# Up projection: eight of 22 steps as seven block products, with weight sums added by transfers

## The chip, the cores and the metric

The kernel runs on one core of one Trainium2 chip. Time is the device time of one launch in microseconds, given as the median of several runs. The core has a matrix engine (TensorE, PE in the profile, with its weight loads as PEld), a vector engine (VectorE, DVE), a scalar engine (ScalarE, ACT), GpSimd (POOL) and SyncE (SP), which issues most of the transfers. Each engine takes its own instructions strictly in the order of its list.

## The reference

One layer over 512 latent rows of width 1024, with 256 context rows: a modulated RMSNorm, one input projection that feeds a two-way state-space mixer and a windowed attention, both merged by gates and projected; then a second modulated RMSNorm, a gated convolutional feed-forward of width 2816, and a final norm.

```python
mod = jax.nn.silu(c) @ w_mod[l] + b_mod[l]
sh1, sc1, gt1, sh2, sc2, gt2 = jnp.split(mod[:, None, :], N_MOD, axis=-1)
...
x = x + gt1 * o_lat          # o_lat = (g_ssd * (y_ssd @ w_o_ssd) + g_att * (y_att @ w_o_att)) @ w_out
x = x + gt2 * conv_ffn(modulate(x, norm2_g[l], sh2, sc2), w_up[l], ffn_conv_w[l], ffn_conv_b[l], w_down[l])
...
def conv_ffn(h, w_up, conv_w, conv_b, w_down):
    u = dwconv_centred(h @ w_up, conv_w, conv_b)      # three taps along the rows
    a, b = u[..., :D_FF], u[..., D_FF:]
    return (jax.nn.silu(a) * b) @ w_down
```

## The kernel before

All products run in two parts for precision: a 32-bit operand is split into a high part (a cast on ACT, `whi`) and a low part (a subtraction on DVE, `wlo`), and each product is three matmuls: high by high, input-low by high, input-high by low. `gemm` issues them for k = 0 to 7 in that order, so the third matmul of a step is the first that reads `wlo`. A weight step is 128 output columns: a load of 512 KB into one of three buffers (`wraw`, issued on SP), the cast, the subtraction (`split`), and 24 matmuls of 512 columns.

The program is one list of steps. `run` walks it and issues the load and the split of a weight one weight ahead of the step that uses it. A scheduler then sets the final order on each engine, except where a block is pinned by hand (`manual_schedule`), or where a manual dependency ties an instruction behind another. `weave` spreads the second list of steps evenly among the first.

The stages that the change touches are these, in the order of the program.
- From the entry on, DRAM to DRAM transfers issued by POOL form sums of down-projection weights (`SUMS`), each a copy and a transfer that adds, tied behind splits by `sum_step`. The down projection already runs as seven block products on them.
- The output projection of the mixer: steps os0 to os7, then out0 to out4 (`out_step`) and `out_last`, which does steps 5, 6 and 7 in halves of 256 rows. Each out step evicts `x` (x1 = old x plus gain times product, on DVE), squares it on ACT and adds the square to `q` on DVE. The squares feed the root of norm 2 (`rs`, on POOL) and its spread over partitions on PE.
- The modulation vectors: `m_step` i forms products of an already loaded weight (`wm`) with the silu of c on DVE, two for every 512 KB (`tm`). Four steps make one group of 512 outputs; groups 2 to 5 are summed over partitions by four transposes on PE and a reduction on DVE, while groups 6 and 7 are summed by `fold`: the tile is stored to DRAM and halved eight times by transfers that add, each waiting for the one before, all on POOL.
- The up projection: 22 steps (`up_step`) of two weights, a (gate) and b, 48 matmuls of 512 columns. Each half is convolved over rows (`conv`: an ACT activation and two DVE sums), a goes through silu, and the product stays for the down projection. `f_sums` forms that projection's column sums. `x1_turn` transposes x1 by blocks and stores it.

What set the amounts woven before:

```python
+ weave([os_step(o) for o in range(3, 8)], msteps[10:18])
+ weave([out_step(o) for o in range(5)], msteps[18:24])
...
weave([up_step(t) for t in range(18)], msteps[24:]) + [up_step(t) for t in range(18, NFF)],
```

## Time and profile before

| | us |
|---|---|
| median of 3 runs (lowest, highest) | 1214.6 (1213.96, 1215.82) |
| the profiled execution | 1214.44 |
| its span | 1212.7 |
| PE busy | 1204.0 |
| DVE busy | 917.3 |
| ACT busy | 684.6 |
| POOL busy | 265.6 |

The mean granted clock of the profiled execution is 0.999. Timeline rows give start, duration, engine, line of the kernel, operation, output<-inputs and count, with the idle time before it and what ended it in brackets. A matmul's own duration is modelled and overlaps the next one's; the distance of two starts is what it costs. Groups of instructions by line give busy time, mean ns of one, and idle time before. Rows of transfers give queue, count, size and the median us from issue to landing.

### The profile page before, as it was taken

The page shows a single profiled execution, that of the slowest core. Times are in us where ns is not written, and L with a number is a line of the kernel's source. Part 1 is how long each engine was busy: PE and PEld are TensorE (multiplying, and loading weights), DVE is VectorE, ACT ScalarE, POOL GpSimd, SP SyncE. Part 2 cuts the span into 40 slices and gives each one's busy share as a digit, 9 for nine tenths or more (in the row PEclk, how much of TensorE's full clock was granted, in tenths as well). Part 3 has the DMA queues.
Part 4 walks back from the last instruction along what each step waited for, and adds up shares of the span by engine and source line. Part 5 has one row for each costly group of instructions (what it writes and reads, how often), then busy time and mean ns, then how long its engine had stood idle before and what let it go on. Part 6 is the DMA issues. An engine that isn't in the chain of part 4 may idle for free.

```text
span 1212.7 us, 17847 instructions
## 1 busy us (share of the span) xinstructions
PE 1204.0 (99%) x6429; PEld 1006.4 (83%) x6429; DVE 917.3 (76%) x1476; ACT 684.6 (56%) x1269; POOL 265.6 (22%) x274
## 2 busy tenths in 40 slices
PE   9999999999999999999999999999999999999998
PEld 6798888888878878788787888888988888888886
DVE  5857887888565588788887977677677777668787
ACT  4657887778543457476575674223544343436654
POOL 0000121100102546265382780000200100110021
PEclk9999999999999999999999999999999999999999
DMA  9655789844747736567467568677265634436652
GB/s 368 257 144 185 161 232 269 169 136 137 170 153 228 229 106 197 162 161 189 147 175 265 178 232 267 223 251 236 53 163 146 200 113 139 130 106 225 213 186 97
DMA packets 129417, 224.30 MB, mean 185 GB/s; under 512 B 27336, under 2 KB 70640, under 8 KB 129328
## 3 DMA queue, kind: packets, MB, share of 16 engines
q1 hardware_dynamic: 115248, 195.61, 51.5%
q0 software_dynamic: 13792, 27.27, 10.0%
q8 instruction: 51, 0.84, 0.3%
q14 instruction: 38, 0.31, 0.1%
q10 hardware_dynamic: 288, 0.27, 0.1%
HBM read 196.17 MB, written 45.02 MB: 199 GB/s over the span
## 4 chain that ended last, share of the span: by engine, by line
PE 93%; DMA 2%; DVE 1%; POOL 1%; issue 1%; ACT 1%; DVEq 0%; POOLq 0%; ACTq 0%
PE acc L238 18%; PE acc L241 18%; PE acc L239 18%; PE score L979 3%; PE po L1028 3%; PE pt L1015 2%; PE mis L582 2%; PE mis L1759 2%; PE mis L1602 2%; DMA xs_d<-xb 2%; PE mis L2310 2%; PE mis L2311 2%; PE mis L2309 2%; PE mis L1767 1%; PE acc L2310 1%; PE acc L2311 1%
## 5 line engine op out<-in xcount | busy, mean ns | idle before, releaser
L184 DVE TENSOR_TENSOR wlo<-wraw,whi 128x1024 fp32r<-128x1024 f32 (+1 forms) x115 | 148.3, 1289 | 87.9 <-ACT whi L183 84.7
L183 ACT CAST whi<-wraw 128x1024 fp32r<-128x1024 f32 (+1 forms) x115 | 120.3, 1047 | 154.0 <-PE acc L239 104.6
L238 PE MATMUL acc<-hlh,whi 128*128 128x512 f32 x472 | 192.8, 409 | 0.0
L241 PE MATMUL acc<-hlh,wlo 128*128 128x512 f32 x472 | 185.6, 393 | 0.0
L239 PE MATMUL acc<-hll,whi 128*128 128x512 f32 x472 | 185.0, 392 | 0.0
L238 PE MATMUL acc<-mh,whi 128*128 128x512 f32 x368 | 143.3, 389 | 0.0
L239 PE MATMUL acc<-ml,whi 128*128 128x512 f32 x368 | 143.2, 389 | 0.0
L241 PE MATMUL acc<-mh,wlo 128*128 128x512 f32 x368 | 143.2, 389 | 0.0
L241 PEld LDWEIGHTS acc<-hlh,wlo 128*128 128x128 f32 x472 | 88.6, 188 | 19.9 <-issue 0.5
L238 PEld LDWEIGHTS acc<-hlh,whi 128*128 128x128 f32 x472 | 88.8, 188 | 17.6 <-issue 2.8
L239 PEld LDWEIGHTS acc<-hll,whi 128*128 128x128 f32 x472 | 88.9, 188 | 17.4 <-issue 2.2
L241 PEld LDWEIGHTS acc<-mh,wlo 128*128 128x128 f32 x368 | 69.1, 188 | 14.4
L239 PEld LDWEIGHTS acc<-ml,whi 128*128 128x128 f32 x368 | 69.1, 188 | 14.3
L238 PEld LDWEIGHTS acc<-mh,whi 128*128 128x128 f32 x368 | 69.1, 188 | 14.2
L164 POOL DMA_DIRECT2D dsum<-wdn x24 | 25.3, 1119 | 194.4 <-DVE wlo L1112 183.7
L988 DVE CUSTOM_DVE_ANT_0 p<-score,winm,nsink 128x512 f32<-128x512 f32 (+1 forms) x64 | 51.9, 810 | 15.3 <-PE score L979 13.8
L995 ACT ACTIVATE p<-p,mneg 128x512 f32<-128x512 f32 (+1 forms) x64 | 49.8, 778 | 15.4 <-DVE mneg L988 14.8
L813 DVE SCALAR_TENSOR_TENSOR tm<-wraw,csil,tm 128x512 f32<-128x512 f32 x56 | 45.8, 818 | 12.2 <-DMA wraw<-wm 11.4
L1023 DVE TENSOR_TENSOR ptl<-pt,pth 128x512 fp32r<-128x512 f32 x72 | 47.5, 686 | 8.5 <-ACT pth L1019 7.7
L238 PE MATMUL acc<-hch,whi 128*128 128x256 f32 x176 | 53.2, 302 | 0.0
L1112 DVE TENSOR_TENSOR wlo<-wraw,whi 128x1024 fp32r<-128x1024 f32 x30 | 36.7, 1223 | 18.3 <-ACT whi L1109 18.0
L241 PE MATMUL acc<-hch,wlo 128*128 128x256 f32 x176 | 49.8, 283 | 0.0
(458 smaller groups left out, 3056.9 us busy)
## 6 DMA issues: line engine op xcount, KB each, us to landing
wraw<-wup SPq DMA_DIRECT2D x44, 512.0 KB, 3.9
dsum<-wdn POOLq DMA_DIRECT2D x24, 704.0 KB, 8.5
wraw<-wm SPq DMA_DIRECT2D x32, 512.0 KB, 4.2
fb<-cs_d SPq DMA_DIRECT2D x32, 512.0 KB, 7.1
wraw<-wx SPq DMA_DIRECT2D x24, 512.0 KB, 4.1
wm<-wm SPq DMA_DIRECT2D x16, 512.0 KB, 8.3
wraw<-wz SPq DMA_DIRECT2D x16, 512.0 KB, 5.0
far<-us_d SPq DMA_DIRECT2D x32, 256.0 KB, 5.3
```

The costliest lines, as they stand in the source:

```text
L183: F["cast"] = S.copy(hi[:, :n], r[:, :n])
L184: F["sub"] = V.tensor_tensor(lo[:, :n], r[:, :n], raw(hi[:, :n]), ALU.subtract)
L238: T.matmul(ps, wh, xh[:, k0 + k, :], start=a, stop=False)
L239: T.matmul(ps, wh, xl[:, k0 + k, :], start=False, stop=False)
L241: T.matmul(ps, wl, xh[:, k0 + k, :], start=False, stop=b)
L813: V.scalar_tensor_tensor(acc, r[:, u * 512 : u * 512 + 512], sc, acc, ALU.mult, ALU.add)
L979: T.matmul(ps[:, o : o + len(z) * P], Q[h][:, b * P : (b + 1) * P], k[:, j, z[0] * P : (z[-1] + 1) * P], start=v == 0 and o % 512 in (0, P ...
L988: V.tensor_tensor_reduce(p[:, :w], d["ps"][i][:, o0 : o0 + w], m, op0=ALU.add, op1=ALU.min, scale=1.0, scalar=nsink[:, h : h + 1], accum_o ...
L995: S.activation(p, p, AF.Exp, bias=d["mneg"][:, i : i + 1], scale=-1.0, accum_out=d["den"][:, i : i + 1])
L1023: V.tensor_tensor(d["ptl"][x], d["pt"][x], raw(d["pth"][x]), ALU.subtract)
L1028: T.matmul(d["po"], vst[:, cols[x], j, :], d[y][x], start=x == 0 and y == "pth", stop=x == c - 1 and y == "ptl")
L1112: sum_step(V.tensor_tensor(d["w"][1], d["r"], raw(d["w"][0]), ALU.subtract), 1 + (4 <= g < 12))
```

## The change

Eight of the 22 up steps (t = 5 to 12) are written as seven products of half-size blocks (weights halved along the contraction and between a and b, inputs along the contraction and the rows): 84 matmuls of 256 columns in place of 48 of 512. Four block sums of weights are formed by adding transfers in DRAM, in three chains that are issued in turn, together with the down sums, two behind each split from the entry on; the host adds a second layout of the same weights (`wup7`) that has no arithmetic in it. Eight of the down sums' transfers (`LATE`) stand behind splits of up steps past 13. Four block sums of the inputs are formed by 7 DVE passes and split by 4 casts and 4 subtractions, in pieces pinned behind splits of up steps 0 to 4. The steps of seven products have their order written out by hand for all four engines, and multiply the two halves on POOL. The column sums of steps up to 17 are formed later, in larger pieces.

The other steps move to make room: the os stage now has modulation steps 10 to 19 (was 10 to 17), the five out steps have 20 to 27 and four of the eight transposes of x1 (was 18 to 23 and none), and up steps 14 to 17 have modulation steps 28 to 31 and the other four transposes (the former were woven into up steps 0 to 17, with the transposes).

In the lists below lines have the numbers of each kernel. On DVE, around the eviction of out step 2 (before, L1984, then after, L2043): `wlo` is the split of the next weight, `mod` and `a` the modulation vector, `tm` the modulation products, `ta<-x` the transposes of x1.

```order
L1984 SCALAR_TENSOR_TENSOR x_7775<-acc,g1h,te 128x512
L184 TENSOR_TENSOR wlo<-wraw,whi 128x1024
L1933 TENSOR_TENSOR q_7777<-q_7777,tc 128x512
L813 SCALAR_TENSOR_TENSOR tm<-wraw,csil,tm 128x512 x4
L1984 SCALAR_TENSOR_TENSOR x_7775<-acc,g1h,te 128x512
```

```order
L2043 SCALAR_TENSOR_TENSOR x_7800<-acc,g1h,te 128x512
L882 TENSOR_REDUCE mod_95<-mis 128x4
L1992 TENSOR_TENSOR q_7802<-q_7802,tc 128x512
L883 TENSOR_TENSOR mod_95<-mod_95,vec 128x4
L870 TENSOR_SCALAR tm<-wraw,csil 128x512
L1981 SCALAR_TENSOR_TENSOR a_7804<-mod_95,vec 128x8
L872 SCALAR_TENSOR_TENSOR tm<-wraw,csil,tm 128x512
L2409 STREAM_TRANSPOSE ta<-x_7800 128x512
L224 TENSOR_TENSOR wlo<-wraw,whi 128x1024
L872 SCALAR_TENSOR_TENSOR tm<-wraw,csil,tm 128x512 x2
L2409 STREAM_TRANSPOSE ta<-x_7800 128x512
L2043 SCALAR_TENSOR_TENSOR x_7800<-acc,g1h,te 128x512
```

Before, the split is the first row behind the eviction; now seven rows stand between. The same holds further on, for out step 3 with one row and for the split of `wlast` with four.

On POOL, around the two roots of norm 2 (`rs`; `ml` is the low part of the normed input), before and after:

```order
L296 TENSOR_TENSOR rs<-ms,phalf 128x4
L296 TENSOR_TENSOR rs<-ms,phalf 128x2
L2026 TENSOR_TENSOR ml<-ta,mh 128x256 x3
L296 TENSOR_TENSOR rs<-ms,phalf 128x2
L2026 TENSOR_TENSOR ml<-ta,mh 128x256 x5
L789 DMA fold_765<-tm 128x512
```

```order
L355 TENSOR_TENSOR rs<-ms,phalf 128x4
L848 DMA fold_768<-tm 128x512
L850 DMA fold_768<-fold_768 256x128
L850 DMA fold_768<-fold_768 128x128
L850 DMA fold_768<-fold_768 64x128
L850 DMA fold_768<-fold_768 32x128
L850 DMA fold_768<-fold_768 16x128
L355 TENSOR_TENSOR rs<-ms,phalf 128x2
L850 DMA fold_768<-fold_768 16x64
L2085 TENSOR_TENSOR ml<-ta,mh 128x256
L850 DMA fold_768<-fold_768 16x32
L2085 TENSOR_TENSOR ml<-ta,mh 128x256
```

The fold of group 6, which stood behind all of norm 2, now has six of its transfers ahead of the first root of two columns.

On DVE, from the end of up step 17 to the split of step 18's first weight (`tc` is the convolution of half b), before and after:

```order
L184 TENSOR_TENSOR wlo<-wraw,whi 128x1024
L2059 SCALAR_TENSOR_TENSOR tc<-acc,vec,tc 128x511
L2060 SCALAR_TENSOR_TENSOR tc<-acc,vec,tc 128x511
L2072 TENSOR_TENSOR fx_8982<-tb,tc 128x512
L2050 SCALAR_TENSOR_TENSOR fx_8981<-fx_8981,fx_8982 128x256
```

```order
L2141 SCALAR_TENSOR_TENSOR tc<-acc,vec,tc 128x511
L2142 SCALAR_TENSOR_TENSOR tc<-acc,vec,tc 128x511
L2154 TENSOR_TENSOR fx_9057<-tb,tc 128x512
L872 SCALAR_TENSOR_TENSOR tm<-wraw,csil,tm 128x512 x2
L224 TENSOR_TENSOR wlo<-wraw,whi 128x1024
```

The split stood ahead of the second half's convolution, and now stands behind it and the last two modulation products.

```diff
-    SUMS = []
-    for j, first_, more in (
-        (4, wdn[0], wdn[2]), (1, wdn[2], wdn[3]), (2, DSUMS[4], wdn[3]), (5, DSUMS[2], wdn[1]),
-    ):
-        cols = [slice(q * DK * P, (q + 1) * DK * P) for q in range(4)]
-        SUMS += [(DSUMS[j][:, c], first_[:, c], {}) for c in cols]
-        SUMS += [(DSUMS[j][:, c], more[:, c], dict(accum_op=ALU.add, max_dma_last_dim=DK * P)) for c in cols]
+    US = dpool.tile([P, 4, len(SEVEN) * 512], F32, name="usum")
+    SUMS, LATE = [], []
+
+    def added(o, x, y):
+        return [(o, x, {}), (o, y, dict(accum_op=ALU.add, max_dma_last_dim=DK * P))]
+
+    def in_turn(runs, n):
+        out, live = [], []
+        runs = list(runs)
+        while runs or live:
+            while runs and len(live) < n:
+                live.append(list(runs.pop(0)))
+            for r in live:
+                out.append(r.pop(0))
+            live = [r for r in live if r]
+        return out
+
+    RUNS = []
+    for q in range(4):
+        c = slice(q * DK * P, (q + 1) * DK * P)
+        two, four = DSUMS[2][:, c], DSUMS[4][:, c]
+        RUNS.append(added(four, wdn[0][:, c], wdn[2][:, c]) + added(two, four, wdn[3][:, c]))
+        RUNS.append(added(DSUMS[1][:, c], wdn[2][:, c], wdn[3][:, c]))
+        LATE.append(added(DSUMS[5][:, c], two, wdn[1][:, c]))
+    for i in range(0, len(SEVEN), 2):
+        c = slice(512 * i, 512 * min(i + 2, len(SEVEN)))
+        a0, a1, b0, b1 = (wup7[:, u, c] for u in range(4))
+        one, two, three, four = (US[:, u, c] for u in range(4))
+        RUNS.append(added(one, b0, b1) + added(two, one, a0) + added(four, two, a1))
+        RUNS.append(added(three, a0, b0))
+    SUMS, LATE = in_turn(RUNS, 3), in_turn(LATE, 4)
...
-    def sum_step(ins, n=1):
+    def sum_step(ins, n=1, SUMS=SUMS):
...
+    def load_sums(key):
+        t = key[1]
+        z = slice(512 * (t - SEVEN[0]), 512 * (t - SEVEN[0]) + 512)
+        if key[0] == "ul":
+            r = wpool.tile([P, 1024], F32, tag="raw", name="wraw", bufs=3)
+            nc.sync.dma_start(r[:, 0:512], US[:, 2, z])
+            nc.sync.dma_start(r[:, 512:1024], wup[NFF + t, :, 512:1024])
+            return r
+        r = F["c3pool"].tile([P, 1024], F32, tag="sraw", name="sraw", bufs=2)
+        if key[0] == "us":
+            nc.sync.dma_start(r.rearrange("p (u n) -> p u n", u=2), US[:, 0:2, z])
+        else:
+            nc.sync.dma_start(r[:, 0:512], US[:, 3, z])
+        return r
...
+    def behind(key):
+        if key[0] == "v" or key == ("q", 1):
+            sum_step(F["sub"], 2)
+        if key[0] == "up":
+            SPLITS[key[1]] = F["cast"], F["sub"]
+            if key[1] % NFF > SEVEN[-1] + 1:
+                sum_step(F["sub"], 1, LATE)
+
+    def pinned(t, casts=(), lows=()):
+        for v, some in enumerate((casts, lows)):
+            for ins in some:
+                tc.add_manual_dep(ins.ins, SPLITS[t][v].ins.name, QUEUED, reason="behind a weight's split")
+
...
-            sum_step(V.tensor_tensor(d["w"][1], d["r"], raw(d["w"][0]), ALU.subtract), 1 + (4 <= g < 12))
+            sum_step(V.tensor_tensor(d["w"][1], d["r"], raw(d["w"][0]), ALU.subtract), 2 if g < 22 else 1)
...
+    def f_sums(p0, p1, pool=False):
+        x, y = F["x"]
+        z = slice(p0, p1)
+        e, f, g, h = (a[:, z, q] for a in (x, y) for q in HALF)
+        W = G if pool else V
+        f_split(0, z, e)
+        W.tensor_tensor(e, e, f, ALU.subtract)
+        f_split(1, z, e)
+        W.tensor_tensor(f, h, f, ALU.subtract)
+        V.scalar_tensor_tensor(e, e, -1.0, h, ALU.mult, ALU.subtract)
+        V.scalar_tensor_tensor(F["t"][:, z, :], e, -1.0, g, ALU.mult, ALU.subtract)
...
+    def input_sum(i):
+        r = F["h2"]
+        b11, b12, b21, b22 = (r[:, HK * a : HK * a + HK, z] for a in range(2) for z in HALF)
+        if i < 3:
+            k, z = ((slice(0, HK), HALF[0]), (slice(HK, KT), HALF[0]), (slice(0, KT, 2), HALF[1]))[i]
+            return V.tensor_tensor(r[:, k, z], raw(h2h[:, k, z]), raw(h2l[:, k, z]), ALU.add)
...
+    def pieces(*todo):
+        def fn():
+            for t, i in todo:
+                if i < 7:
+                    pinned(t, (), (input_sum(i),))
+                else:
+                    s, v = input_split(i - 7)
+                    pinned(t, (s,), (v,))
+
+        return [], fn
...
+    def seven(t, j):
+        part = lambda key, h: [v[:, 512 * h : 512 * h + 512] for v in B[key, t]]
+        if j == 5:
+            B["x", t], B["y", t] = accb(), misb()
+            w, b, ps = part("us", 0), 0, B["y", t]
+        elif j == 1:
+            w, b, ps = part("a", 0), (0, 0), B["x", t]
+        elif j == 2:
+            B["z", t] = misb()
+            w, b, ps = part("a", 1), (1, 0), B["z", t]
+        elif j == 3:
+            w, b, ps = B["u4", t], (1, 1), B["y", t]
+        elif j == 6:
+            w, b, ps = part("us", 1), 1, B["x", t]
+        else:
+            w, b, ps = part("ul", int(j == 4)), 2 if j == 7 else 3, B["x", t]
+        if isinstance(b, int):
+            of = lambda v, k: F["T"][:, v, b, k * HL : k * HL + HL]
+        else:
+            of = lambda v, k: (h2h, h2l)[v][:, HK * b[0] + k, HALF[b[1]]]
+        for k in range(HK):
+            wh, wl = (x[:, k * P : k * P + P] for x in w)
+            st, en = k == 0 and j in (1, 2, 5), k == HK - 1 and j in (2, 3, 4)
+            T.matmul(ps[:, :HL], wh, of(0, k), start=st, stop=False, skip_group_check=True)
+            T.matmul(ps[:, :HL], wh, of(1, k), start=False, stop=False, skip_group_check=True)
+            T.matmul(ps[:, :HL], wl, of(0, k), start=False, stop=en, skip_group_check=True)
+
...
+    def quarter(t, n):
+        p = B.get(("p", t))
+        if n == 11:
+            B["ca", t] = tmp("ta")
+            V.tensor_tensor(B["ca", t][:, HALF[0]], p[:, HALF[1]], B["z", t][:, :HL], ALU.add)
+        elif n == 3:
+            S.copy(B["ca", t][:, HALF[1]], B["y", t][:, :HL])
+        elif n == 12:
+            V.tensor_tensor(B["ca", t][:, HALF[1]], B["x", t][:, :HL], B["ca", t][:, HALF[1]], ALU.add)
+        elif n == 22:
+            B["cb", t] = tmp("tc")
+            V.scalar_tensor_tensor(B["cb", t][:, HALF[1]], p[:, HALF[0]], -1.0, B["x", t][:, :HL], ALU.mult, ALU.subtract)
+        else:
+            S.activation(B["cb", t][:, HALF[0]], B["x", t][:, :HL], AF.Copy, scale=-1.0)
...
+    def put_up(t):
+        G.tensor_tensor(F["x"][t % 2][:, t // 2, :], B["oa", t], B["ob", t], ALU.mult)
...
+    def seven_step(t):
+        n, a, b = t + 1, t - 1, t - 2
...
+            with tc.manual_schedule(engines=EVERY):
+                if old:
+                    quarter(a, 12)
+                seven(t, 5)
+                if new:
+                    sum_cast("us", n)
+                if older:
+                    conv_rest("b", b, NFF + b)
+                    put_up(b)
+                if old:
+                    conv_first("a", a, a, "tb")
+                kept_half(t, 0, B["y", t])
+                if new:
+                    sum_low("us", n)
+                seven(t, 1)
+                if new:
+                    whole_cast(n)
+                kept_half(t, 1, B["x", t])
+                if old:
+                    conv_rest("a", a, a)
+                    seven(a, 7)
+                if new:
+                    sum_cast("u4", n)
+                sum_cast("ul", t)
+                if old:
+                    quarter(a, 22)
+                if new:
+                    whole_low(n)
+                if old:
+                    silu_a(a)
+                seven(t, 2)
+                quarter(t, 11)
+                if new:
+                    sum_low("u4", n)
+                sum_low("ul", t)
+                seven(t, 3)
+                quarter(t, 3)
+                if old:
+                    seven(a, 4)
+                    quarter(a, 21)
+                    conv_first("b", a, NFF + a, "tm")
+                seven(t, 6)
+
...
-            t = tmp("te")
-            V.transpose(t, x1[c // 4][:, c % 4, :])
+            t = tmp("te" if c > 3 else "ta")
+            tc.keep_in_program_order(V.transpose(t, x1[c // 4][:, c % 4, :]))
...
-        + weave([os_step(o) for o in range(3, 8)], msteps[10:18])
-        + weave([out_step(o) for o in range(5)], msteps[18:24])
+        + weave([os_step(o) for o in range(3, 8)], msteps[10:20])
+        + weave(
+            [out_step(o) for o in range(5)],
+            msteps[20:23] + [x1_turn(0)] + msteps[23:25] + [x1_turn(1), msteps[25], x1_turn(2)] + msteps[26:28] + [x1_turn(3)],
+        )
         + [([], vectors)]
         + [([("out", o) for o in (5, 6, 7)], out_last), ([], close_c1)]
+        + [up_step(0), pieces((1, 0)), up_step(1), pieces((NFF + 1, 1), (2, 2))]
+        + [up_step(2), pieces((NFF + 2, 3), (3, 4)), up_step(3), pieces((NFF + 3, 7), (4, 5), (4, 6))]
+        + [up_step(4), pieces((NFF + 4, 8)), seven_in(SEVEN[0]), pieces((NFF + 4, 9), (NFF + 4, 10))]
+        + [seven_step(t) for t in SEVEN]
+        + [seven_out(SEVEN[-1] + 1)]
         + weave(
-            weave([up_step(t) for t in range(18)], msteps[24:]) + [up_step(t) for t in range(18, NFF)],
-            [([], lambda: None)] * 6 + [x1_turn(c) for c in range(8)] + [x1_rows] + [([], lambda: None)] * 6 + [([], row_tiles)],
+            [up_step(t) for t in range(SEVEN[-1] + 2, 18)],
+            [([], lambda: f_sums(0, 2))] + [x1_turn(c) for c in (4, 5)] + [([], lambda: f_sums(2, 4))]
+            + [x1_turn(c) for c in (6, 7)] + msteps[28:] + [x1_rows],
+        )
+        + weave(
+            [up_step(t) for t in range(18, NFF)],
+            [([], lambda p=p: f_sums(p, min(p + 2, DK))) for p in (4, 6, 8, 10)] + [([], row_tiles)],
         )
         + [down_step(j, u) for j in range(7) for u in range(3 if j == 6 else DU)],
         early=("g", 15),
     )
+
+
+SEVEN = range(5, 13)
```

145 lines of the change are left out of this document (123 added, 22 removed).

## The prediction

> **What bounds the kernel now.** I read first the busy times and the chain of the page, then the waits of the matrix engine, then the timeline of the stages that the change rewrites.
>
> ```profile
> PE 1204.0 (99%) x6429; PEld 1006.4 (83%) x6429; DVE 917.3 (76%) x1476; ACT 684.6 (56%) x1269; POOL 265.6 (22%) x274
> PEclk9999999999999999999999999999999999999999
> PE 93%; DMA 2%; DVE 1%; POOL 1%; issue 1%; ACT 1%; DVEq 0%; POOLq 0%; ACTq 0%
> ...
> PE mis L460 <- DVE ones L443: 1.0, 1, 1.0
> PE mis L1621 <- DVE xw L1590: 1.0, 1, 1.0
> PE acc L241 <- DVE wlo L184: 0.4, 1, 0.4
> ```
>
> PE is busy in 99% of the span, carries 93% of the chain, and its longest wait is 1.0 us. So time can go only by taking matmul work away, and every wait that a new order puts before a matmul is added in full: there is no slack on PE to take it. The sum below is made against the profiled execution, 1214.44 us, 0.16 us under the median of 1214.6.
>
> **Term 1, seven block products.** What a matmul costs is the distance between starts, not its own modelled length.
>
> ```profile
> 836.02 0.39 PE L241 MATMUL acc<-mh,wlo 128*128 128x512 f32 x1
> 836.25 0.39 PE L238 MATMUL acc<-mh,whi 128*128 128x512 f32 x1
> ...
> 839.53 0.28 PE L1942 MATMUL acc<-ml,wlast 128*128 128x256 f32 x1
> 839.65 0.28 PE L1943 MATMUL acc<-mh,wlast 128*128 128x256 f32 x1
> ```
>
> 512 columns cost 0.227 us (836.02 to 836.25, over many rows), 256 columns 0.120 us (839.53 to 839.65). An up step of 48 matmuls of 512 takes 48 x 0.227 = 10.90 us; seven products of 12 matmuls of 256 take 84 x 0.1198 = 10.06 us. Eight such steps: 8 x 0.84 = **-6.7 us**. Not the quarter less that the count of products promises (7 of 8 would be 1.36 us a step): a 256-wide matmul costs 53% of a 512-wide one.
>
> The cover of the extra vector work is PE's 10.06 us a step:
>
> ```profile
> 880.00:931.00 51.00, 51.00 (x226) 42.24 (x225) 39.04 (x59) 20.58 (x28) 0.00 (x0) 1.00 0.61 156
> ...
> L2039 DVE TENSOR_TENSOR fs<-fx,fs 128x256 fp32r<-128x256 f32 x22 | 9.2, 420 | 4.3 <-ACT fs L2038 4.3
> L2060 DVE SCALAR_TENSOR_TENSOR tc<-acc,vec,tc 128x511 f32<-128x511 f32 x22 | 16.5, 749 | 0.7
> L2072 DVE TENSOR_TENSOR fx<-tb,tc 128x512 f32<-128x512 f32 x22 | 15.2, 691 | 0.7
> ```
>
> In the window (columns: stretch, its length, busy PE, PEld, DVE, ACT, POOL) DVE works 39.0 of 51 us on up steps. A step of seven products gives DVE three splits of 1024 (1.22 each), one of 512 (0.69), four conv sums (0.78 with issue) and three quarter sums of 256 (0.42): 3.66 + 0.69 + 3.12 + 1.26 = 8.7 us of 10.06. ACT has three casts of 1.05, one of half that, four 256-wide copies and three 512-wide activations, some 7.5 us. The products of the last step (POOL) and the deferred column sums have over 10 us before anyone reads them. So I cost all that at 0. If the cover is gone, each step returns to what DVE needs, at most the 0.84 us gained. In steps 1 to 4, where the input sums are pinned, DVE comes near PE's 43.5 us: 0.77 of it by the share above is 33.3, less 4.2 of deferred column sums (ten of 0.42), plus 11 passes of 1.22 is 42.5. I take 0, at worst 2 us.
>
> **Term 2, the output stage.** Twice as many modulation products and four transposes of x stand on DVE in these five steps, and the order puts the split of the next out weight behind them.
>
> ```profile
> 822.15 0.60 PE L821 MATMUL mis<-ident,tm 128*128 128x128 f32 x4
> 822.51 0.49 PE L238 MATMUL acc<-mh,whi 128*128 128x512 f32 x1
> ...
> 823.06 0.39 PE L241 MATMUL acc<-mh,wlo 128*128 128x512 f32 x1
> ...
> 814.68 0.68 DVE L1874 TENSOR_TENSOR ml<-tb,mh 128x512 fp32r<-128x512 f32 x1
> 815.28 1.53 DVE L813 SCALAR_TENSOR_TENSOR tm<-wraw,csil,tm 128x512 f32<-128x512 f32 x2
> ...
> 822.36 0.75 DVE L1984 SCALAR_TENSOR_TENSOR x<-acc,g1h,te 128x512 f32<-128x512 f32 x1 [3.32 <-PE acc L241]
> 823.02 0.68 DVE L823 TENSOR_REDUCE mod<-mis 128x4 f32<-128x512 f32 x1
> 823.62 1.22 DVE L184 TENSOR_TENSOR wlo<-wraw,whi 128x1024 fp32r<-128x1024 f32 x1
> 824.75 0.69 DVE L1933 TENSOR_TENSOR q<-q,tc 128x512 f32<-128x512 f32 x1
> 825.36 0.15 DVE L824 TENSOR_TENSOR mod<-mod,vec 128x4 f32<-128x4 f32 x1
> 825.43 0.48 DVE L811 TENSOR_SCALAR tm<-wraw,csil 128x512 f32<-128x512 f32 x1
> 825.95 2.33 DVE L813 SCALAR_TENSOR_TENSOR tm<-wraw,csil,tm 128x512 f32<-128x512 f32 x3
> ...
> 822.17 1.05 ACT L183 CAST whi<-wraw 128x1024 fp32r<-128x1024 f32 x1 [3.83 <-PE acc L239]
> 823.14 0.63 ACT L1932 ACTIVATE tc<-x 128x512 f32<-128x512 f32 x1
> ...
> L2120 DVE STREAM_TRANSPOSE te<-x 128x512 f32<-128x512 f32 x8 | 5.6, 704 | 0.0
> ...
> wraw<-wm SPq DMA_DIRECT2D x32, 512.0 KB, 4.2
> ```
>
> Write E for the start of PE's next work after an out step (822.15 here). The step's eviction x starts at E+0.21. The next step's third matmul is the first to read wlo, at E+0.91 behind four transposes, at E+0.45 without. Starts on DVE follow one another by 0.66 (x), 0.60 (reduce), 0.61 (q), 0.07, 0.52 (tm), 0.07, 0.78 (tm), 0.65 (transpose, 0.70 less overlap).
> - Split for out step 3, now behind x, reduce, q, mod, tm, a, tm, transpose: the square that q needs ends at E+1.62, so 1.62 + 0.61 + 0.07 + 0.52 + 0.07 + 0.78 + 0.65 = 4.32, end 5.54. Against 0.91: **+4.6**.
> - Out step 4, behind x and q; ACT takes the square before the cast: 1.62 + 1.05 + about 1.35 = 4.0, against 0.45: **+3.6**.
> - Out steps 5 to 7 (wlast), behind x, tm, q, tm, transpose: 0.21 + 0.66 + 0.78 + 0.61 + 0.78 + 0.65 = 3.7, end 4.9, against 0.32: **+4.6**.
> - Out step 2: its load takes the buffer of modulation weight 21, read behind the last ml of the stage before: 814.68 + 0.60 + 3 x 0.78 = 817.6; load 4.2 to 5 (two at once), cast 1.05, split 1.2: 824.6 to 825.9 against 822.7. **+2.7** (0 to 4). Out step 0's ml, with DVE nearly full in front of it: **+1** (0 to 3).
>
> Here the queue behind the waiting split holds the next products and transposes, which PE does not need, so a wait does not grow.
>
> **Term 3, the fold on POOL.** Modulation group 6 now ends in the output stage, and its fold, nine transfers that each wait for the one before, stands in POOL's order ahead of the root of norm 2.
>
> ```profile
> 838.98 0.60 PE L821 MATMUL mis<-ident,tm 128*128 128x128 f32 x4
> 854.49 0.38 PE L302 MATMUL mis<-ident,rs 128*128 128x128 f32 x2
> ...
> 852.39 0.70 POOL L296 TENSOR_TENSOR rs<-ms,phalf 128x2 f32<-128x2 f32 x1 [111.99 <-DVE ms L295]
> ...
> 946.20 0.63 POOL L789 DMA_DIRECT2D fold<-tm  x1 [73.42 <-DVE tm L813]
> 951.90 0.98 POOL L791 DMA_DIRECT2D fold<-fold  x1 [5.06 <-DMA fold<-tm]
> ...
> 966.71 0.76 POOL L791 DMA_DIRECT2D fold<-fold  x1 [2.18 <-DMA fold<-fold]
> ```
>
> From the first issue to the end of the sixth are 966.71 + 0.76 - 946.20 = 21.3 us. Before, nobody waits for this. Now the first issue waits for the last tm, at E+3.1 after out step 4, and the root (0.70) comes behind the sixth: E+3.1+21.3+0.75 = E+25.2. PE wants the spread 854.49 - 838.98 = 15.5 us after E, less 0.35 (four transposes gone), plus the 4.6 of the wlast wait: E+19.75. **+5.4**. The remaining fold transfers alternate with the eight ml pieces, second root included: **+0.4** (0 to 0.8).
>
> **Term 4, up step 17 to 18.** Before the split of step 18's first weight DVE now has the whole second half of step 17 and the last modulation product; ACT's cast stands behind the activation (0.77, from E+0.21). Then two sums (0.78 each), the product (0.74), two tm (0.78 each), split: 1.0 + 1.56 + 0.74 + 1.56 + 1.22 = 6.1, against E+0.45: **+5.6**. More if the modulation weight, queued on SP behind small writes of x, is late.
>
> **Other edits, at 0.** The weight sums:
>
> ```profile
> dsum<-wdn POOLq DMA_DIRECT2D x24, 704.0 KB, 8.5
> ```
>
> There are 32 more transfers of 512 KB. Two are issued per split, three chains deep, so a transfer of 8.5 us is spread over steps of 7 to 11 us, and weight loads of 4.2 us are asked for a step ahead. Free if that lead holds; if it fails for a few loads near the entry, a late load costs 1 to 2 us: 0 to 4. The roots' and x's stores on POOL behind them come some 50 us later. More x transposes, f sums in larger pieces and LATE sums lie under PE: 0 to 1.
>
> **Sum.** -6.7 + 4.6 + 3.6 + 4.6 + 2.7 + 1.0 + 5.4 + 0.4 + 5.6 = +21.2, so 1214.44 + 21.2 = **1235.6 us**.
>
> **Rivals.**
> - The waits are hidden: the other side. If DVE, ACT and POOL had reached those rows ahead of PE, only term 1 is left: 1214.44 - 6.7 = 1207.7. It decides once terms 2 to 4 sum to under 6.7. Against it: in the rows above DVE cannot pass x before PE's last matmul (3.32 us idle, released by PE), and an engine takes its rows in order.
> - Half of the waits: the fold's transfers go faster than 21.3 us (by over 5 us the wait is gone, -5.4), or the loads of term 2 are early (-3.7), or step 18's split is not late: 1222 to 1231.
> - The matrix engine restarts slowly after each new idle time.
>
> ```profile
> 1.04 4.64 PE L460 MATMUL mis<-ones 128*128 128x128 f32 x20 [1.04 <-DVE ones L443]
> ...
> 8.03 1.58 PE L460 MATMUL mis<-ones 128*128 128x128 f32 x12
> ```
>
> After the idle start 20 matmuls take 0.232 us each, at 8.03 twelve of the same kind 0.132. If each of the five waits of 3.6 to 5.6 us were followed by such a stretch, some 3.4 us at half rate lose 1.7 us: 5 x 1.7 = 8.5, so up to 1244. Against it: the granted clock reads 9 tenths in the first slice too, and no wait inside the span is over 1.0 us, so nothing here shows it after a wait. The Trainium skill, "TensorE: Matmul & The Clock Gate", section "What's actually happening", states this rule: after one idle window of about 3.4 us the array runs at half clock until it was busy for about as long. The windows run free, so by it a wait of 4.6 us need not hold a whole one; an estimate from that page is two of the five, 3 to 4 us, and a time of 1239. I keep the sum without it, since the waits are the larger unknown.
> - The change doesn't do what it says: DVE sets the seven-product steps, the 6.7 us don't come, and the waits stay: 1242.
>
> **Chances.** Forecast 0.50; half of the waits 0.17; slow restart 0.18; no gain 0.05; hidden 0.07; the remaining 0.03 a balance near zero. Faster by over 0.2% (2.4 us, what a measurement can tell) 0.07, same 0.03, slower 0.90. The range: 1222 (half of the waits, low end) to 1247 (slow restart with late loads), leaving the hidden case, the balance and the edges of the others outside.
>
> **What will show it.** In the changed profile: PE rows of steps 5 to 12 at 0.120 us a matmul and 10.1 us a step; waits of PE on wlo, wlast and mis in the output stage of 3 to 5 us each, the one at the spread released by POOL's root with "DMA fold" ahead of it; a wait of 5 to 6 us on wlo at step 18. Wrong would be: no such waits, or steps of 11 us bound by DVE, or loads late between 53 and 326 us.

## The result, and the profile after

The changed kernel takes 1260.3 us (1257.6 to 1262.3), the kernel before 1214.75 us on the same chip. The ratio is 1.037 (95% interval 1.035 to 1.040): slower by 45.5 us, where 21.2 were forecast, and beyond the range's end at 1247. The profiled execution of the changed kernel took 1262.33 us with a span of 1260.5, so its trace is 2.0 us over the median. From the page, in the order in which the prediction showed them for before:

```profile
PE 1216.5 (97%) x6717; PEld 1024.8 (81%) x6717; DVE 948.0 (75%) x1489; ACT 709.1 (56%) x1311; POOL 313.5 (25%) x314
PEclk9998999999999999999999999998999999899999
PE 78%; DMA 11%; DVE 6%; ACT 2%; issue 2%; POOL 2%; SPq 0%; DVEq 0%; POOLq 0%; ACTq 0%
...
dsum<-wdn POOLq DMA_DIRECT2D x24, 704.0 KB, 10.7
```

PE's share of the chain fell from 93% to 78%, and transfers now carry 11% of it. The granted clock, 9 tenths in all 40 slices before, has three slices at 8. The transfers that read the down weights for their sums land after 10.7 us, 8.5 before. What PE waited for, by releaser (us in total, times, longest):

```profile
PE acc L297 <- ACT whi L223: 14.8, 4, 9.3
PE mis L361 <- POOL rs L355: 5.2, 1, 5.2
PE acc L300 <- DVE wlo L224: 4.1, 6, 1.6
PE score L1038 <- DVE mneg L1047: 3.7, 1, 3.7
PE acc L2000 <- ACT wlast L223: 2.5, 1, 2.5
PE acc L2002 <- DVE wlast L224: 1.7, 1, 1.7
```

These are 32.0 us where the longest wait had been 1.0. To place the loss I compared the start of the same matmul in both traces. The shift grows like this:

| stretch | predicted | measured |
|---|---|---|
| entry, to 131 us | 0 (0 to 4) | +9.6 |
| attention and mixer, to the output stage | 0 | +1.9 |
| out steps 0 to 2 | +3.7 | +2.4 |
| out steps 3 and 4, `wlast`, the spread | +18.2 | +24.2 |
| second norm, to up 1 | +0.4 | +0.5 |
| up 1 to 14, seven block products | -6.7 | -6.3 |
| up 17 to 18, and into 19 | +5.6 | +9.6, +5.9 |
| rest | 0 | 0 |
| sum | +21.2 | +47.8 |

The seven products run as priced, one start each 0.12 us:

```profile
960.06 0.28 PE L2269 MATMUL mis<-mh,ringrbc 128*128 128x256 f32 x1
960.18 0.28 PE L2270 MATMUL mis<-ml,ringrbc 128*128 128x256 f32 x1
```

**The entry.** The transfers issued from 80 to 130 us (count, KB each, median us to landing), first before, then after:

```profile
dsum<-wdn POOLq DMA_DIRECT2D x6, 704.0 KB, 5.4
wraw<-wz SPq DMA_DIRECT2D x4, 512.0 KB, 4.2
```

```profile
dsum<-wdn POOLq DMA_DIRECT2D x10, 704.0 KB, 13.0
wraw<-wz SPq DMA_DIRECT2D x3, 512.0 KB, 10.4
```

Then windows of 4 us in the trace of after (length; busy PE, PEld, DVE, ACT, POOL; granted clock; share of the DMA engines; GB/s):

```profile
104.00:108.00 4.00, 0.46 (x2) 0.03 (x1) 1.82 (x3) 2.24 (x4) 0.17 (x1) 0.92 1.11 289
108.00:112.00 4.00, 3.87 (x11) 3.29 (x12) 0.99 (x5) 2.40 (x5) 0.94 (x2) 0.50 1.16 238
112.00:116.00 4.00, 4.00 (x17) 3.49 (x17) 2.41 (x4) 3.85 (x9) 0.52 (x1) 0.73 1.15 262
```

And two rows of ACT, from the timeline:

```profile
65.15 0.69 ACT L703 ACTIVATE tb<-mis,gb 128x512 f32<-128x512 f32 x1 [3.80 <-DMA ts_d<-tb]
...
105.10 1.04 ACT L1168 CAST whi<-wraw 128x1024 fp32r<-128x1024 f32 x1 [5.09 <-DMA wraw<-wq]
```

All 16 DMA engines are full, loads take over twice as long, a weight arrives 5 us after ACT was ready for it, DVE's split and the softmax behind it are late, and PE stands for 3.8 us. Then the clock is granted at half, and the next 6.2 us cost 2.9 more. Another 3.3 us were lost before, between 65 and 69 us, right behind the first sums: ACT waits 3.8 us for a store that still reads its buffer (the first row; it did not wait there in the kernel before), and the casts of the input pieces behind it are late. With 0.4 us gained ahead of that, these make the 9.6.

**The output stage, the spread and up 18.** PE's waits and the rows that release them (start, us, engine; idle time and releaser in brackets):

```profile
844.57 0.77 PE L297 MATMUL acc<-mh,whi 128*128 128x512 f32 x1 [2.00 <-ACT whi L223]
847.35 0.79 PE L300 MATMUL acc<-mh,wlo 128*128 128x512 f32 x1 [1.58 <-DVE wlo L224]
857.02 0.50 PE L297 MATMUL acc<-mh,whi 128*128 128x512 f32 x1 [2.50 <-ACT whi L223]
867.67 0.39 PE L2000 MATMUL acc<-mh,wlast 128*128 128x256 f32 x1 [2.50 <-ACT wlast L223]
869.86 0.58 PE L2002 MATMUL acc<-mh,wlast 128*128 128x256 f32 x1 [1.68 <-DVE wlast L224]
892.60 0.69 PE L361 MATMUL mis<-ident,rs 128*128 128x128 f32 x2 [5.24 <-POOL rs L355]
...
891.02 0.76 POOL L850 DMA_DIRECT2D fold<-fold  x1 [4.00 <-DMA fold<-fold]
891.55 0.99 POOL L355 TENSOR_TENSOR rs<-ms,phalf 128x2 f32<-128x2 f32 x1
...
1076.07 15.80 SPq L2412 DMA_DIRECT2D x_d<-te  x12
1091.97 2.36 SPq L217 DMA_DIRECT2D wraw<-wm  x1
1094.38 0.43 SPq L217 DMA_DIRECT2D wraw<-wup  x1
...
1099.02 1.04 ACT L223 CAST whi<-wraw 128x1024 fp32r<-128x1024 f32 x1 [7.37 <-DMA wraw<-wup]
1100.12 0.80 PE L297 MATMUL acc<-mh,whi 128*128 128x512 f32 x1 [9.29 <-ACT whi L223]
```

The root for the spread stands right behind the fold, as forecast. Up 18 was forecast wrongly: not a long row of vector work, but SP (the engine whose queue issues the loads), held for 15.8 us by twelve small stores of x, issues that step's weight so late that ACT has nothing to cast until 1099. DVE's rows set nothing there: it sat idle for 0.78 us ahead of the split, waiting for that cast.

### The profile page after: what moved, and what is told of

Read it like the earlier page. It is cut to its first block, busy times and chain, and to the rows that moved or that the text cites. A ratio compares the mean times of both kernels' runs of the same rounds, so it can differ in the third digit from the quotient of the medians.

```text
span 1260.5 us, 18593 instructions
## 1 busy us (share of the span) xinstructions
PE 1216.5 (97%) x6717; PEld 1024.8 (81%) x6717; DVE 948.0 (75%) x1489; ACT 709.1 (56%) x1311; POOL 313.5 (25%) x314
## 4 chain that ended last, share of the span: by engine, by line
PE 78%; DMA 11%; DVE 6%; ACT 2%; issue 2%; POOL 2%; SPq 0%; DVEq 0%; POOLq 0%; ACTq 0%
PE acc L300 13%; PE acc L297 13%; PE acc L298 13%; PE score L1038 3%; PE po L1087 3%; PE pt L1074 2%; PE mis L1818 2%; PE mis L641 2%; PE mis L1661 2%; DMA wraw<-wm 2%; DMA xs_d<-xb 2%; PE mis L2599 2%; PE mis L2598 2%; PE mis L2600 2%; DVE wlo L224 1%
## 5 line engine op out<-in xcount | busy, mean ns | idle before, releaser
L223 ACT CAST whi<-wraw 128x1024 fp32r<-128x1024 f32 (+1 forms) x99 | 103.1, 1043 | 131.0 <-PE acc L298 56.1
L224 DVE TENSOR_TENSOR wlo<-wraw,whi 128x1024 fp32r<-128x1024 f32 (+1 forms) x99 | 129.3, 1307 | 61.5 <-ACT whi L223 61.2
L297 PE MATMUL acc<-mh,whi 128*128 128x512 f32 x240 | 97.1, 405 | 15.4 <-ACT whi L223 14.8
L300 PE MATMUL acc<-mh,wlo 128*128 128x512 f32 x240 | 97.0, 404 | 3.1 <-DVE wlo L224 3.1
L298 PE MATMUL acc<-ml,whi 128*128 128x512 f32 x240 | 96.3, 401 | 0.8 <-DVE ml L1933 0.8
L297 PEld LDWEIGHTS acc<-mh,whi 128*128 128x128 f32 x240 | 46.9, 195 | 26.8 <-ACT whi L223 16.3
L300 PEld LDWEIGHTS acc<-mh,wlo 128*128 128x128 f32 x240 | 46.6, 194 | 15.8 <-DVE wlo L224 6.1
L298 PEld LDWEIGHTS acc<-ml,whi 128*128 128x128 f32 x240 | 46.9, 195 | 10.9 <-DVE ml L1933 1.2
L298 PE MATMUL acc<-hcl,whi 128*128 128x256 f32 x176 | 50.1, 285 | 0.7 <-DVE hcl L635 0.5
L189 POOL DMA_DIRECT2D usum<-wup x24 | 25.1, 1129 | 99.4 <-DVE wlo L1171 89.9
## 6 DMA issues: line engine op xcount, KB each, us to landing
dsum<-wdn POOLq DMA_DIRECT2D x24, 704.0 KB, 10.7
```

What stands on the lines that cost most here:

```text
L223: F["cast"] = S.copy(hi[:, :n], r[:, :n])
L224: F["sub"] = V.tensor_tensor(lo[:, :n], r[:, :n], raw(hi[:, :n]), ALU.subtract)
L297: T.matmul(ps, wh, xh[:, k0 + k, :], start=a, stop=False)
L298: T.matmul(ps, wh, xl[:, k0 + k, :], start=False, stop=False)
L300: T.matmul(ps, wl, xh[:, k0 + k, :], start=False, stop=b)
```

## Experiments

My theory after the comparison: four separate places lose time (the crowded entry, the order of the output stage, the fold, SP's queue before up 18), and each long wait costs a slow restart on top. Rivals: what is saved in one place is lost in the next, or the added transfers cost time wherever they stand. `before` is 1213.5 to 1214.7 us beside all runs.

**1. Sums start at the q weights.**

```
-  if key[0] == "v" or key == ("q", 1): sum_step(F["sub"], 2)
-  sum_step(V.tensor_tensor(ws[n][1], ...), n * 2)
+  V.tensor_tensor(ws[n][1], ...)
-  sum_step(V.tensor_tensor(d["w"][1], ...), 2 if g < 22 else 1)
+  sum_step(V.tensor_tensor(d["w"][1], ...), 2)
```

> The change with the weight sums' transfers begun at the split of the ninth input weight (about 92 us), as before, instead of at the entry; two behind every split from there on. Theory 'traffic': the transfers between 54 and 107 us made the load of a q weight late; then the 9.6 us that the entry lost go, and the time is 1251 (1249 to 1253), with no wait of PE over 1 us before 130 us. Rival 'the entry lost its time elsewhere': unchanged, 1258 to 1262. If later sums meet the next stage instead, part of the 9.6 us comes back between 110 and 330 us.

1258.45 us, ratio 1.036 (1.034 to 1.038). The entry's shift falls from +9.6 to +0.5, so the transfers were its cause. But the time misses the 1251 expected: 5.5 us come back between 194 and 720 us in waits of 0.6 to 1.5 us, the "part comes back" of the expectation.

**2. The last four transposes of x in up steps 18 to 21, one a step.**

```
-  [f_sums(0, 2)] + [x1_turn(4), x1_turn(5)] + [f_sums(2, 4)] + [x1_turn(6), x1_turn(7)] + ...
+  [f_sums(0, 2), f_sums(2, 4)] + msteps[28:]          # and one x1_turn in each of ups 18 to 21
```

> The change with the last four transposes of x1 and their 16 stores moved from up steps 14 to 17 to up steps 18 to 21, one a step. Theory 'SP queue': the weight load of step 18 stood behind 12 stores that held SP from 1076 to 1092 us; without them the 15.5 us lost at steps 18 and 19 go: 1245 (1243 to 1247). Theory of the prediction, 'DVE order' (the split behind the half's convolution and two products): 5.6 us, so no more than that can come back if the load stays late: 1254.

1260.68 us, 1.037 (1.036 to 1.039). The wait at up 18 falls from 9.45 to 3.1 us, so the stores cause most of it; the 3.1 us end with the split, which stands on DVE behind a modulation product whose weight came 2.6 us late. Ups 18 and 19 lose 6.1 us instead of 15.5, but the time stays, far from the 1245 expected: the down projection loses 11.7 us, with waits of 2.9 and 3.9 us for casts, since its loads now stand behind the late stores. (The traced execution took 1266.23 us, the longest of five.)

**3. The fold behind the second norm's last piece.**

```
+  tc.add_manual_dep(first.ins, F["ml"].ins.name, QUEUED, reason="behind norm 2")   # first transfer of fold(6)
+  ... up_step(0), pieces((1, 0)), ([], lambda: fold(6, F["acc6"])), up_step(1) ...               # called here
```

> The change with the fold of group 6 issued on POOL behind the last low part of norm 2, not ahead of the root. Theory: the wait of 5.2 us at the spread goes, and the slow stretch behind it (892 to 896 us at 0.57 of the clock, some 1.5 us): 1253 (1252 to 1255). If the slow stretch stays because the earlier waits cause it: 1255. Rival 'the root is late through the squares, not the fold': unchanged, 1260.

1250.15 us, 1.030 (1.028 to 1.031). The spread waits for nothing. The shift after the second norm is +31.5 instead of +38.7: the wait of 5.4 us and the slow stretch behind it are gone, while 1.5 of the difference was there ahead of the output stage already.

**4. The same, and the output stage's splits ahead of the products.** `ahead` is raised by 2 for the out weights, and the products and transposes stand behind the split.

> The change with the fold of group 6 behind norm 2 (as in e3) and, in the output stage, three weights loaded ahead and the modulation products and transposes tied on DVE behind the split of the next out weight. Theory 'DVE order': of the waits before out step 3 (4.9 us), out step 4 (3.7) and wlast (4.5) the first two go, the third falls to about 2, and the slow stretches behind them go with them (about 5 us of 7): e3's 1250 less 10 to 16, so 1235 to 1240. Rival 'the loads, not the order': the waits stay, 1250.

1252.16 us, 1.031 (1.030 to 1.032): nothing gained. With DVE's order out of the way, ACT's casts wait for the loads themselves:

```profile
842.54 1.04 ACT L223 CAST whi<-wraw 128x1024 fp32r<-128x1024 f32 x1 [3.67 <-DMA wraw<-wout]
852.20 1.04 ACT L223 CAST whi<-wraw 128x1024 fp32r<-128x1024 f32 x1 [6.04 <-DMA wraw<-wout]
```

**5. The kernel of 4 without transposes in the output stage** (they and their 16 stores go to ups 0 to 3).

> The kernel with the late fold and the splits ahead in the output stage, with one more edit: the four transposes of x and their 16 stores leave the output stage for ups 0 to 3; the two modulation weights a step stay there. Theory (two modulation weights and the output weight a step share three buffers, and that makes the loads late): the waits of ACT on the load of the output weight stay, 1250 us. Rival (the stores of x on SP's queue delay the loads' issue): those waits go, and with them their slow clock, about 1240 us.

1244.24 us, 1.024 (1.023 to 1.026). The output stage still loses 16.9 us (4: 21.7), and ACT still waits for the out weight:

```profile
847.54 1.04 ACT L223 CAST whi<-wraw 128x1024 fp32r<-128x1024 f32 x1 [6.68 <-DMA wraw<-wout]
```

The time lies between the two expectations: the transposes and their stores carry a part, and most of the rest points at two modulation weights a step, which share three buffers with the out weight. In the runs 7 to 10, where the output stage has its old list, it loses 0. These differ from 5 in more than that (they do not load three weights ahead), so the share of the modulation weights is inferred, not isolated.

**6. Stores of the last four transposes issued by POOL.**

```
-  nc.sync.dma_start(o, t[32 * a : 32 * a + 32, :]...)
+  (G if c > 3 else nc.sync).dma_start(o, t[32 * a : 32 * a + 32, :]...)
```

> The change with one edit: the stores of the last four transposes of x are issued by POOL, not by SP. Theory 'SP queue': the loads of step 18's weights come on time, the split then stands ahead of the half's convolution in DVE's order, and all of the 15.5 us go: 1245. Rival 'DVE order' of the prediction alone: the wait stays at 5.6 us and its slow stretch: 1252. If x's rows are then read late on SP, some of it returns at steps 19 to 21 or in the down projection.

1256.63 us, 1.034 (1.032 to 1.036). Up 18 and 19 lose nothing (-13.7 us against the changed kernel in the trace), and 9.2 come back when the down projection reads the last modulation group, whose fold POOL issues behind the stores; its first transfer lands 16.5 us later. With the load on time the split stands ahead of the half's convolution on DVE again, so this run puts no price on the order that the prediction had named. POOL's timeline:

```profile
1091.03 2.59 POOL L2412 DMA_DIRECT2D x_d<-te  x4 [2.46 <-DVE te L2409]
1095.55 1.28 POOL L848 DMA_DIRECT2D fold<-tm  x1
1113.31 0.92 POOL L850 DMA_DIRECT2D fold<-fold  x1 [16.48 <-DMA fold<-tm]
```

PE's wait for it:

```profile
PE mis L2436 <- DVE g2c L2434: 6.5, 1, 6.5
```

**7. Old output stage, late stores on POOL, sums apart.** Output stage and mixer get their old lists, modulation steps 24 to 31 go to ups 14 to 19; transposes 0 to 3 go to ups 0 to 3, 4 to 7 to ups 16 to 19, with the stores of the latter issued by POOL; 40 of the sums start at 92 us, 16 stand in ups 1 to 8, 8 in ups 14 to 17.

> The eight steps of seven products with the rest put back or apart: sums from 92 us on, 40 transfers in that stretch and the last 16 of the up sums behind splits of up steps 1 to 4 and inside steps 5 to 8; os and output stages with the modulation steps of before; transposes of x in up steps 0 to 3 and 16 to 19, the last four's stores issued by POOL; modulation steps 24 to 31 in up steps 14 to 19; the rows of gains after ten down steps. Theory 'every loss came from placement, none from the seven products': the 6.4 us gained stand nearly alone, 1208 to 1211. Rival 'the sums cost wherever they stand' (e1 lost 5.5 us between 194 and 720 us): 1213 to 1216.

1224.45 us, 1.010 (1.008 to 1.012). The shift is 0 at the entry, +1.6 up to the output stage, 0 in it; the seven products give only 3.6, and ups 16 to 20 lose 10.8, with the DMA engines' share at 1.05 where the late sums stand.

**8. The late sums brought forward.** All 32 sums of down weights in 92 to 326 us, 24 of the up weights' behind the splits of x's weights (345 to 600 us), 8 in ups 1 to 4.

> The seven-product steps stay as in the run with the sums spread apart. Of the transfers, all 32 that sum down weights run at the kernel before's pace in 92 to 326 us, 24 of the up weights' transfers come one behind each split of x's weights (345 to 600 us), and the last 8 behind the splits of the first four up steps, none inside the seven-product steps and none in ups 14 to 19. Theory (the loss was the crowding of transfers and stores at the entry, in the output stage and in ups 16 to 20): nothing is lost before up 4, the seven-product steps give back their 6.3 us, and nothing is lost after them: 1208 to 1210 us. Rival (the added transfers cost 2 to 5 us wherever they stand, or the transposes and stores still make PE wait in ups 14 to 19, each wait over 4 us with a slow clock of 1.3 to 2.7 us behind it): 1213 to 1218 us, with waits in one of those two places.

1227.04 us, 1.011 (1.010 to 1.013). Ups 14 to 19 now lose 0.7, the seven products give 6.3, but 18.1 us go before 720 us. PE's two longest waits there, 2.5 us at 414 and 2.8 at 601, lie behind loads that land late: four loads of the mixer (`fb`, 512 KB) after 16.4 us in the median where they had taken 10.6, a modulation weight after 8.7 where it had taken 4.9 (timeline of ACT, DVE and PE):

```profile
409.98 0.70 ACT L1783 ACTIVATE E<-fb,TX 128x128 f32<-128x128 f32 x2 [5.45 <-DMA fb<-cs_d]
...
599.36 0.75 DVE L872 SCALAR_TENSOR_TENSOR tm<-wraw,csil,tm 128x512 f32<-128x512 f32 x1 [5.09 <-DMA wraw<-wm]
...
600.86 1.10 PE L1661 MATMUL mis<-xw,Bk 128*128 128x512 f32 x2 [2.81 <-DVE xw L1649]
```

**9. None behind x's weights.** 48 sums two to a split in 92 to 331 us, 16 in ups 1 to 4.

> The kernel of the run with the sums behind x's weights, with one edit: none of the 64 added transfers stands behind a split of x's weights. 48 (all 32 of the down weights, 16 of the up weights) are issued two behind each split in 92 to 326 us, and the other 16 two behind each split of ups 1 to 4. Theory (a transfer that waits at the head of POOL's queue holds POOL's own work in 390 to 620 us, the bytes as such cost nothing): the 18 us lost up to 720 us fall to 1.6, the seven-product steps give back 6.3 to 7, and the kernel takes 1207 to 1210 us, less than before. Rival (the transfers' bytes cost some us wherever they stand): 3 to 8 us are lost in 92 to 390 us or in ups 1 to 4, and it takes 1213 to 1218 us.

1217.26 us, 1.0025 (1.0008 to 1.0041). 4.2 us are lost before the output stage instead of 18.1, so where they stood was most of the price. That POOL's list made it, as the expectation had it, is not shown: in 8 it was late loads, and the wait left at 207 us (2.2 us) is one for a small transfer of the attention (`q`). 3.8 are lost in up 0, where a transfer that adds to the sum just ahead of it waits for that one, with the norm's pieces (ml) behind it on POOL (timeline of POOL and PE):

```profile
874.89 1.34 POOL L189 DMA_DIRECT2D usum<-wup  x1 [3.31 <-DMA usum<-wup]
...
877.03 0.58 PE L2165 MATMUL acc<-ml,whi 128*128 128x256 f32 x1 [3.19 <-POOL ml L2083]
```

**10. Spaced at those two places.** One transfer instead of two behind the splits at 190 to 209 us; the last 16 in ups 2 to 4, four chains in turn.

```
-  SUMS, UPS = in_turn(RUNS[:12], 3) + in_turn(LATE, 4), RUNS[12] + RUNS[13] + RUNS[14] + RUNS[15]
+  SUMS, UPS = in_turn(RUNS[:12], 3) + in_turn(LATE, 4), in_turn(RUNS[12:], 4)
-  2)
+  2 - (8 < g < 12))
```

> The run with the sums early, with one edit to where its transfers stand: behind the three splits at 190 to 209 us one transfer instead of two; behind none of the splits issued before up 1 begins, and the last 16 three behind each split of ups 2 to 4, in four chains in turn so that no transfer waits for the one just ahead of it. Theory (what is left is queue holding: the wait of 2.36 us at 207 us with 1.9 of slow clock, and the wait of 3.36 us in up 0 with 1.5 behind it): 4 to 8 us go, 1209 to 1213 us. Rival (the bytes themselves cost it, and the waits only move): 1215 to 1218 us.

1214.77 us, 1.0002 (0.9993 to 1.0011): as long as before, and over the 1209 to 1213 expected. Both waits are gone (shift +1.9 up to the output stage, none added in up 0). But the seven products give only 1.2: a wait of 2.74 us and 1.4 of slow clock stand in the first of them. PE waits there for a buffer that ACT empties behind the cast of a summed weight; SP issued that weight at 915.39, and it landed 8.0 us later (3.5 in the changed kernel), with the DMA engines full of the last sums and of stores of x. The window, and the rows of SP and ACT:

```profile
920.00:924.00 4.00, 2.23 (x19) 2.03 (x17) 3.31 (x4) 0.99 (x2) 0.55 (x1) 1.00 1.12 307
```

```profile
915.39 0.37 SPq L202 DMA_DIRECT2D sraw<-usum  x1
...
923.44 1.04 ACT L2229 CAST ringa<-sraw 128x1024 fp32r<-128x1024 f32 x1 [3.01 <-DVE tc L2140]
```

The row names DVE, but the weight had landed only 0.1 us before. Whether the sums or the stores carry this wait was not tried; if the sums do, the rival's "the waits only move" holds.

**11 and 12. Waits put into the kernel before.** In chosen up steps a chain of 256-wide adds on POOL, which PE has to wait for, stands between the two halves:

```
+  y = tmp("te")[:, :HL]; S.activation(y, pa[:, :HL], AF.Copy, scale=0.0)
+  for _ in range(n): G.tensor_tensor(y, y, y, ALU.add)
+  T.transpose(misb()[:, :P], y[:, :P], ident)
```

> The kernel before, with nine waits put between the two halves of up steps 2, 3, 4, 9, 10, 11, 12, 20, 21: PE transposes a tile that POOL adds to itself 3, 6, 1, 2, 4, 5, 8, 3, 4 times, some 0.75 us each, so waits of about 1.5 to 7 us. The transposed tile is not used. 'Plain waits': each costs its own length, and matmuls start 0.227 us apart right behind it. 'Slow restart': behind waits over about 3.4 us (four adds or more) matmuls start 0.45 us apart for 2 to 3.5 us, 1 to 1.7 us more for each, with the granted clock at 0.5 there; shorter waits cost their length alone.

> As w1, on the kernel before, with the copy that starts the chain ahead of the activation of the first half, and other counts: 1, 2, 3, 4, 5, 6 adds in up steps 1 to 6, then 3, 5, 2, 4 in steps 12 to 15, 3 and 4 in steps 20 and 21; waits of about 1.5 to 5 us. 'Plain waits': only their length. 'Slow restart' by a window of 3.4 us that runs free: waits under 3 us cost nothing more, waits of 3.4 to 6.8 us sometimes 1.7 us more, as the window falls.

One execution each: 1307.77 us with nine waits of 5.5 to 11.0 us, 1289.28 with twelve of 1.3 to 6.3. All nineteen of 4.06 us and more were followed by 1.3 to 2.7 us lost in matmuls at half rate; the two shorter ones, 1.34 and 3.49 us, by 0.1. In the second run, two starts behind the wait of 3.49 us, then two behind that of 4.83 (timeline of PE), and the windows of both places:

```profile
894.61 0.40 PE L239 MATMUL acc<-ml,whi 128*128 128x512 f32 x1
894.84 0.40 PE L241 MATMUL acc<-mh,wlo 128*128 128x512 f32 x1
...
911.25 0.63 PE L241 MATMUL acc<-mh,wlo 128*128 128x512 f32 x1
911.68 0.63 PE L238 MATMUL acc<-mh,whi 128*128 128x512 f32 x1
```

```profile
894.00:898.00 4.00, 3.80 (x17) 3.17 (x18) 0.43 (x1) 0.63 (x1) 0.15 (x1) 1.00 0.38 132
910.00:913.00 3.00, 2.87 (x8) 2.30 (x9) 1.01 (x2) 0.63 (x1) 0.07 (x1) 0.50 0.58 194
```

The distance of 0.23 us becomes 0.43, at a granted clock of 0.50.

## Why the prediction was right and wrong

**Right, within half a microsecond a term:** term 1 (-6.3 for -6.7, and DVE's work under it cost nothing), and the order terms, taken as gaps between PE's starts over the usual distance: out step 3 2.2 + 2.0 us (4.6 forecast), step 4 2.7 + 0.7 (3.6), `wlast` 2.7 + 1.8 (4.6), the spread 5.4 (5.4). Experiment 3 shows the fold's mechanism. For the output steps the size held, but two things in it were not as worked out. PE stood first for the cast on ACT (844.57, 857.02, 867.67), which stands behind the square of x and which the working had for step 4 alone, and only then for the split; the sum held because the split still came last. And 4 and 5 show that with the splits put first the loads are late instead, so nothing is gained.

**Small misses:** out step 0's ml cost 2.1 for 1.0. Out step 2 waited 0.6 us for its weight, not 2.7: its load came earlier than the sum had it, and the rows given there add up to 824.1 to 824.9 against 822.7, so to 1.3 to 2.2 and not to 2.7.

**Wrong, the step that priced the sums at 0.** It compared a transfer's landing time with the steps' length, one chain at a time, and forgot that ten of them queue beside the loads of the entry. Measured: +9.6 at the entry, of which 3.3 go at 65 to 69 us, 3.8 are one wait and 2.9 the clock behind it. Experiment 1 shows the cause. 8 to 10 show that where the transfers stand sets most of the price: 18.1, 4.2 and 1.9 us before the output stage. The waits in their traces lie behind loads that land late beside the sums, and in up 0 of run 9 behind a waiting transfer on POOL. No arrangement made the sums free.

**Wrong, term 4, by its engine.** It counted DVE's rows (5.6). The wait was 9.45 and its after-effect brought 15.5 in all, because SP's queue was late. The prediction named those small writes as "more if", and gave them no size. Experiment 6, one change, takes all of it away. What DVE's order alone would have cost stays open.

**Wrong, the slow restart left out of the sum.** It was the third rival, with a chance of 0.18 and a price of 8.5 us, and it came in full: in the changed kernel seven stretches at half the clock cost 14.7 us between the starts of the same matmuls (2.9 at the entry, 8.0 in the output stage and behind the spread, 3.8 in ups 18 and 19). The argument against it, that no wait over 1.0 us was there to show it, was an absence of evidence. The Trainium skill, "TensorE: Matmul & The Clock Gate", section "What's actually happening", states the rule: half the clock after an idle window of about 3.4 us, in windows that run free. The traces agree on the half rate (0.43 us between starts for 0.23) and on windows of 3.41 us, but PE need not be idle for a whole one: being busy for less than 45% of it was enough (last section). So my estimate, two of five waits, was too low: all five places paid (from 844.62, 858.27, 868.51, 892.41 and 1093.79 us on), and in 11 and 12 nineteen of nineteen waits from 4.06 us up.

So 47.8 = 21.2 (forecast) + 9.6 (entry) + 9.9 (up 18 and 19) + 6.0 (out step 3 to the spread: 6.6 of slow clock, waits 0.6 under the forecast) + 1.1 (the small ones). The saving is real, 6.3 us in the trace, but no arrangement tried kept it: with the best, 10, waits and the slow clock take as much. Whether an order exists that keeps it stays open.

## What to carry to other kernels

When the matrix engine is busy in 99% of the span, price an edit by the queues it lengthens (the SP and POOL lists, the load buffers, the DMA engines' share in that stretch) before the arithmetic that it saves: 6.3 us saved, 54 lost. Add to each wait forecast above 4 us some 1.3 to 2.7 us for the slow clock behind it, and reckon with it from 2 us on, where it comes or not as the wait falls. Ask which loads a new transfer will run beside, and put one that must wait for something only on a list where nothing urgent stands behind it.

## What was not expected of the hardware

- The clock is decided window by window, and a window need not be idle to lose it. In the clock records of all fourteen traces, the half-rate stretches of one trace begin whole multiples of 3.413 us apart. Cut into such windows (from 41 us on), the traces have 62 windows at the full clock in which recorded matmuls keep PE busy for less than 45%: all 62 are followed by one at half. Of 20 windows with 45 to 56%, 5 are; of 4708 with more, none. A window at half is followed by a full one when PE is busy for 81% of it or more (67 of 67), and otherwise not (43 of 43). Matmul ends are modelled, so the shares are rough. A wait of some 1.9 us is thus enough if it falls into one window, and one over 3.8 us always is. The wait of 2.0 us before 844.57 lay in one window of the changed kernel, and the clock was at half from 844.62 on; the wait of 3.49 us in 12 fell into two, and cost nothing more. First the one window, then the two (the second number is PE's busy time, the granted clock the third from the end):

```profile
841.21:844.62 3.41, 1.41 (x10) 0.97 (x8) 2.35 (x5) 1.56 (x2) 0.00 (x0) 1.00 0.80 299
```

```profile
889.33:892.74 3.41, 1.54 (x7) 0.94 (x5) 2.48 (x5) 2.00 (x3) 0.65 (x1) 1.00 0.29 117
892.74:896.16 3.42, 1.96 (x9) 1.66 (x10) 1.66 (x3) 0.63 (x1) 1.33 (x2) 1.00 0.47 153
```

- The issue of a small store is not a fixed price. SP's stores of x (issue in ns, least, median, most), before and, for the second half, after:

```profile
L2123 SPq DMA_DIRECT2D x_d<-te x32: 303/480/1483, 860.8 to 935.8; - x32
```

```profile
L2412 SPq DMA_DIRECT2D x_d<-te x16: 303/672/2887, 1054.0 to 1090.5; - x16
```

Twelve of the latter, 15.8 us in a row, are 1.3 us each. What made them longer was not taken apart.
